# One more unit of transposes by DMA, and another order of the transfers behind the last load, in a bf16 time-mixing kernel

## The chip, the cores and the metric

One core of a Trainium2 chip runs the program. The metric is the device time of one execution in microseconds (us); before the change the median of four runs is 202.88 us (202.57 to 203.16). A smaller time is better.

## What is computed

For x of 16 batches x 2048 positions x 256 channels (f32), with x_prev the same rows shifted by one position inside a batch:

```
xv = x * time_mix_v + x_prev * (1 - time_mix_v)
xr = x * time_mix_r + x_prev * (1 - time_mix_r)
out = (sigmoid(xr @ receptance_weight) * (xv @ value_weight)) @ output_weight
```

The key path of the reference doesn't reach the output, and the kernel doesn't compute it.

## The kernel before, in words

**Units.** The work is cut into 64 units of 512 positions (NU = 64), four to a batch, so that unit 44 is the first of batch 11. In the main loop (L522) step g computes unit g: on TensorE (PE) the receptance matmuls into psum_r, the value matmuls into psum_v (both L287) and the output matmuls of an earlier unit into psum_o (L311); on ScalarE (ACT) the sigmoid (L535) and the copy of psum_o to o_sb (L345); on VectorE (DVE) the product z_sb (L580). psum_r, psum_v and psum_o have one buffer each, so PE can't begin the next group of a kind before ACT or DVE has read the last one.

**Mixing.** The matmuls need the channels on the partitions. `xt[b]` holds batch b transposed, in 17 slots of 128 columns for 128 positions x 2 channel halves: slots 1 to 16 are the batch's rows p*16+j by their j, and slot 0 holds the x_prev of slot 1, which is slot 16 moved by one column. The mixed input is a scaled slice of `xt` (DVE L257, POOL L267, and from unit 40 on for the value half ACT L514) plus the slice one slot further (DVE L279). Mixing works on pairs of units and runs one to three units ahead of the matmuls. Slot 0 is made from slot 16: for batches 11 to 15 by a small copy on ACT (L550) in step 4*(b-1)+1, so for batch 11 in step 41, for batch 12 in step 45 and for batch 14 in step 53. ACT takes its instructions in order.

**Two ways to transpose.** For the first 44 units PE transposes x_bf against an identity (L207, eight 128x128 matmuls for a unit) and ACT copies the result to `xt` (L223). The last five batches (BYDMA = 20 units) are transposed from x_bf to `xt` by DMA (`by_dma`, L188, the crossbar). `advance` runs the transposes some six units ahead; because CROSS = 38 is subtracted once in its limit, they stand in steps 36 (unit 42) and 38 (unit 43), and none in step 37. Within a batch from 2 on a unit's transposes are taken in the order of slots 13-16, 1-4, 5-8, 9-12, so unit 43 brings slots 9 to 12 of batch 10 (j = 8 to 11).

**Queues.** SyncE (SP) issues all crossbar transfers and nearly all stores, in program order, to one hardware queue. Loads of x go by POOL's queue. The last load (batch 15) is in two halves. A store moves two units (1 MB); some are kept back (WAITING) so that they don't stand among the transposes. Behind the last loads SP's order is: store of units 32-33 once the first half of the last load has landed; then, once the second half has landed, batch 11 in two transfers (slots 13-16, then 1-12), batch 12, the store of units 34-35, batch 13, four stores, batch 14, batch 15, four stores and so on. Batch 11 is issued in step 38, batches 12, 13, 14 and 15 in steps 39, 43, 47 and 51. `o_sb` and `xt` have three buffers, one batch each.

**Other names that hang on CROSS.** From step LATE_O + 1 = 39 on the output matmuls of unit g-2 stand at the start of step g, where before it those of unit g-1 stood at its end; step 38 has none. From FREE = 38 on ACT scales one channel half of the value input, for even units, in even steps.

Of the kernel before, what the change touches and what calls it, by code (L numbers as in the profile page):

```python
# [15 lines left out]
def kernel(  # L16
# [25 lines left out]
    nc = tc.nc  # L42

    B, S, D = x.shape
    P = 128
    KO = D // P
    J = S // P
    UJ = 4
    TU = UJ * P
    UB = J // UJ  # L50
# [2 lines left out]
    BYUNIT = 2  # L53
    LONG = 8
    H = UJ // 2
    BYDMA = 5 * UB
    CROSS = NU - BYDMA - LOOK
    FREE = CROSS
    LATE_O = CROSS
    WAITING = {33: 38, 35: 39, 37: 43, 39: 43, 45: 51, 47: 51}  # L60
    START_T = [1, 3, 5, 6, 7, 9, 11, 12]
    AHEAD = 6
    PAIRS = 10
# [18 lines left out]
    kept = {}  # L82
# [20 lines left out]
    def load(b):  # L103
        if b not in x_bf:
            x_bf[b] = xpool.tile([P, J, D], BF16, name="x_bf")
        if b < BYUNIT:
            for e in range(UB):
                nc.gpsimd.dma_start(
                    out=x_bf[b][:, e * UJ : (e + 1) * UJ, :], in_=unit_rows(x, b, e)[:, 0]
                )  # L110
            return
        if b < B - 1:
            run = 8192 if b < LONG else 16384
            return nc.gpsimd.dma_start(out=x_bf[b], in_=rows(b), max_dma_last_dim=run)  # L114
        return [
            nc.gpsimd.dma_start(out=x_bf[b][:, j : j + J // 2], in_=rows(b)[:, j : j + J // 2])
            for j in (0, J // 2)
        ]
# [67 lines left out]
    def by_dma(b, lo, hi, after=None):  # L186

        op = nc.sync.dma_start_transpose(  # L188
            out=xt[b][:, 1 + lo : 1 + hi].rearrange("p j k c -> p (j k) c"),
            in_=x_bf[b][:, lo:hi].rearrange("p j d -> p (j d)"),  # L190
        )
        if after is not None:
            tc.add_manual_dep(op.ins, after.ins.name, SYNC, reason="not beside a load")

    def transposes(i):

        b, e = divmod(i, UB)
        if b > 0 and e == 0:
            new_xt(b)
        if b >= BYUNIT:  # L200
            e = (e - 1) % UB
        j0 = 1 + e * UJ + (e if b < BYUNIT else 0)
        if b < BYUNIT or e == UB - 1:
            late_copies.append((b, e))

        def one(ps, jj, ko, src, idn):
            nc.tensor.transpose(  # L207
                out=ps[:, jj], in_=src[:, jj, ko * P : (ko + 1) * P], identity=idn
            )

        if i in (1, 2):
            for ko in range(KO):
                ps = ps_t_pool.tile([P, UJ, P], FP32, name="ps_t")
                for jj in range(UJ):
                    one(ps, jj, ko, x_unit[:, i], ident_f)
                nc.scalar.copy(out=xt[b][:, j0 : j0 + UJ, ko, :], in_=ps)
            return
        ps = ps_t_pool.tile([P, UJ, KO, P], BF16, name="ps_t")
        src = x_bf3 if b == 0 else x_bf[b][:, e * UJ : (e + 1) * UJ, :]
        for jj in range(UJ):  # L220
            for ko in range(KO):
                one(ps[:, :, ko], jj, ko, src, ident)
        nc.scalar.copy(out=xt[b][:, j0 : j0 + UJ], in_=ps)  # L223
# [71 lines left out]
    def project_unmixed(ps, mo):  # L295


        parts = [(w_prev[:, ko], ko, 0) for ko in range(KO)]
        parts += [(w_bf[:, 0, ko], ko, 1) for ko in range(KO)]
        for n, (w, ko, lo) in enumerate(parts):  # L300
            nc.tensor.matmul(
                out=ps[:, mo, :],
                lhsT=w[:, mo * P : (mo + 1) * P],
                rhs=xt[0][:, lo : lo + UJ, ko],
                start=(n == 0),
                stop=(n == len(parts) - 1),
            )
# [11 lines left out]
    def store(queue, b, lo, hi, after=None):  # L319
        dst = out[b].rearrange("(p j) d -> p j d", p=P)  # L320
        op = queue.dma_start(out=dst[:, lo:hi, :], in_=o_sb[b][:, lo:hi, :])
        if after is not None:
            tc.add_manual_dep(op.ins, after.ins.name, SYNC, reason="in turn with the last load")
# [9 lines left out]
    def output(g, z):  # L333
# [20 lines left out]
        elif e % 2 == 1:  # L354
            pair = (b, j0 - UJ, j0 + UJ)
            if g in WAITING:
                kept.setdefault(WAITING[g], []).append(pair)
            else:
# [46 lines left out]
    def pieces(g):  # L405

        b, e = divmod(g, UB)
        tile_for(g // 2)
        return [(b, m, e * TU, (e + 1) * TU) for m in range(2)]
# [21 lines left out]
            tc.add_manual_dep(op.ins, after.ins.name, SYNC, reason="one at a time")  # L431

    tnext = 1
    half_load = last_load = None

    def advance(limit):
        nonlocal tnext, half_load, last_load
        while tnext <= min(limit, NU - 1):
            b, e = divmod(tnext, UB)
            if b == 1 and e > 0:  # L440
                load(b + e + 1)
            elif b > 1 and e == 0 and b + 5 < B:
                if b == 2:
                    load(6)
                last_load = load(b + 5)
                if b + 5 == B - 1:
                    half_load, last_load = last_load
            if tnext < NU - BYDMA:
                transposes(tnext)
            tnext += 1  # L450
# [71 lines left out]
    for g in range(NU - 1):  # L522
        ps_r = ps_r_pool.tile([P, KO, TU], FP32, name="psum_r")
        if g == 0:
            project_unmixed(ps_r, 0)
            advance(1)
            project_unmixed(ps_r, 1)
            for ko in range(KO):
                wrap_slots(pieces(1)[0], ko)
                scale(pieces(1)[0], (ko,))  # L530
            last = add(pieces(1)[0])
        else:
            project(ps_r, g, 0)
        s_sb = zpool.tile([P, KO, TU], BF16, name="s_sb")
        nc.scalar.activation(out=s_sb, in_=ps_r, func=ACT.Sigmoid)  # L535
        advance(START_T[g] if g < len(START_T) else g + LOOK - (g == CROSS - 1))
        for b in range(B - 5, B):
            if g == max(UB * (b - 2) - 1, CROSS + (b > B - 5)):
                new_xt(b)
                if b == B - 5:  # L540
                    for pair in kept.pop(g):
                        store(nc.sync, *pair, after=half_load)
                    by_dma(b, J - UJ, J, last_load)
                    by_dma(b, 0, J - UJ, last_load)
                else:
                    by_dma(b, 0, J)
                for pair in kept.pop(g, []):
                    store(nc.sync, *pair)
            if g == UB * (b - 1) + 1:
                nc.scalar.copy(out=xt[b][:, 0, :, 1:P], in_=xt[b][:, J, :, 0 : P - 1])  # L550
        if LATE_O < g < NU - 2:
            output(g - 2, z_prev2)
        for p in products.get(g + 1, []):
            if g >= FREE and p[0][1] == 1:
                scale_act(p[0], (0,))
        for p in [q for q, _ in products[g]] + pooled[g]:
            last_unit_of = p[3] // TU - 1
            need = last_unit_of if p[0] < BYUNIT else min(last_unit_of + 1, UB - 1)
            assert UB * p[0] + need < tnext, (g, p, tnext)
            if g > AHEAD or p not in pooled[g]:  # L560
                wrap_slots(p)
        if g == 1:
            scale_act(pieces(2)[1], (1,))
        for p, kos in products[g]:
            if not (g - 1 >= FREE and p[1] == 1):
                scale(p, kos)
        for p in sums[g]:
            last = add(p)
        for p in pooled[g]:
            if p[0] >= BYUNIT:  # L570
                wrap_slots(p)
        ps_v = ps_v_pool.tile([P, KO, TU], FP32, name="psum_v")
        project(ps_v, g, 1)
        if g == 0:
            scale_act(pieces(1)[1], (0,))
            advance(2)
        z_sb = zpool.tile([P, KO, TU], BF16, name="z_sb")
        n = TU // 2 if g == NU - 2 else TU
        for c in range(0, TU, n):
            nc.vector.tensor_tensor(  # L580
                out=z_sb[:, :, c : c + n],
                in0=s_sb[:, :, c : c + n],
                in1=ps_v[:, :, c : c + n],
                op=ALU.mult,
            )
        for p in pooled[g]:
            wrap_slots(p, after=last)
            scale_pool(p, last)
        for p in held[g]:
            add(p)  # L590
        if z_prev is not None and not LATE_O <= g < NU - 3:
            output(g - 1, z_prev)
        if g == 1:
            advance(4)
        z_prev2, z_prev = z_prev, z_sb
# [31 lines left out]
```

## Time and profile before

| what | value |
|---|---|
| median of 4 runs | 202.88 us |
| the profiled execution's own time | 202.57 us |
| its span, first to last instruction | 200.5 us |
| granted TensorE clock | full throughout |
| PE transposes L207 | x328 |
| ACT copies of them L223 | x36 (and x5 for the first batches) |
| one ACT copy of psum_o, L345 | 1018 ns |
| crossbar transfers L188 | x6 |
| HBM read and written | 34.34 MB and 33.55 MB |

A row of the timeline gives the start in us from the span's beginning, the duration, the engine ("SPq" is SyncE's instruction stream, where a DMA's duration is the time of its issue and not of its transfer), the line of the kernel, the operation, and out<-in by the program's names. In brackets stands how long the engine was idle before it and who released it. The ends of matmuls are modelled and overlap the next ones, so on PE the distance from one start to the next is what counts. Step g can be found by its sigmoid on ACT: step 36 at 121.98, step 37 at 125.03, step 38 at 127.63, step 41 at 135.50, step 45 at 146.03 and step 53 at 167.11.

### The profile page before, as it was taken

How to read it: one execution, taken by the hardware profiler on the slowest of the kernel's cores; microseconds unless marked ns; L12 is line 12 of the kernel's file. 1: busy time of each engine (PE TensorE's matmuls, PEld its weight loads, DVE VectorE, ACT ScalarE, POOL GpSimd, SP SyncE). 2: the span in 40 equal slices, each digit the busy share in tenths (PEclk: the TensorE clock that was granted, in tenths of full speed). 3: DMA queues.
4: the chain of work that ended last, by engine and by line, in shares of the span. 5: the costliest groups of instructions: out<-in, count | busy, mean ns of one | idle time of the engine just before them, and what ended most of it. 6: DMA issues, size and time to landing. Idle time of an engine off the chain costs nothing.

```text
span 200.5 us, 3891 instructions
## 1 busy us (share of the span) xinstructions
PE 195.3 (97%) x1422; PEld 125.7 (63%) x1422; DVE 186.0 (93%) x296; ACT 180.3 (90%) x202; POOL 83.7 (42%) x115
## 2 busy tenths in 40 slices
PE   8999999999999999999999999999999999999993
PEld 6666676666666666666666666655666565555671
DVE  0999999999999999999999999999999999999982
ACT  3599899999999999999999999899999999999982
POOL 1756572443543534425433354443344444444200
PEclk9999999999999999999999999999999999999999
DMA  5999999999999999999999999899999999999575
GB/s 155 301 175 216 234 279 273 280 281 274 293 311 292 288 280 284 291 280 278 289 288 337 289 409 285 284 193 232 280 270 420 310 224 279 417 422 391 222 308 215
DMA packets 32298, 57.26 MB, mean 286 GB/s; under 512 B 21780, under 2 KB 23064, under 8 KB 28312
## 3 DMA queue, kind: packets, MB, share of 16 engines
q1 hardware_dynamic: 28208, 40.77, 59.7%
q0 software_dynamic: 3920, 16.12, 40.0%
q8 instruction: 11, 0.18, 0.4%
q10 hardware_dynamic: 152, 0.13, 0.2%
q14 instruction: 7, 0.06, 0.1%
HBM read 34.34 MB, written 33.55 MB: 339 GB/s over the span
## 4 chain that ended last, share of the span: by engine, by line
PE 84%; DMA 5%; DVE 5%; issue 2%; ACT 2%; POOL 0%; SPq 0%; DVEq 0%
PE psum_v L287 25%; PE psum_o L311 25%; PE psum_r L287 24%; PE ps_t L207 8%; DMA x_bf<-in_x_dram 3%; DMA w_f<-n_receptance_weight_dram 2%; DVE z_sb L580 2%; DVE mix L279 2%; PE ps_t L311 1%; DVE mix L257 1%; ACT s_sb L535 1%; ACT mix L514 1%; ACT xt L223 1%; PE ps_t L287 0%; SPq L128 0%
## 5 line engine op out<-in xcount | busy, mean ns | idle before, releaser
L267 POOL TENSOR_SCALAR mix<-xt,c_sb 128x1024 bf16<-128x1024 bf16 (+1 forms) x55 | 61.0, 1109 | 92.6 <-DVE mix L279 80.6
L580 DVE TENSOR_TENSOR z_sb<-s_sb,psum_v 128x1024 bf16<-128x1024 bf16 (+1 forms) x64 | 76.7, 1200 | 3.9 <-PE psum_v L287 1.5
L279 DVE TENSOR_TENSOR mix<-mix,xt 128x1024 bf16<-128x1024 bf16 x112 | 77.0, 696 | 1.6
L287 PEld LDWEIGHTS <-w_bf 128*128 128x128 bf16 x516 | 48.7, 98 | 38.3 <-issue 0.7
L535 ACT ACTIVATE s_sb<-psum_r 128x1024 bf16<-128x1024 f32 x63 | 65.0, 1032 | 3.5 <-PE psum_r L287 2.7
L345 ACT COPY o_sb<-psum_o 128x1024 f32<-128x1024 f32 x60 | 61.1, 1018 | 7.2 <-PE psum_o L311 7.0
L287 PE MATMUL psum_v<-mix,w_bf 128*128 128x512 bf16 (+1 forms) x256 | 65.3, 377 | 0.3 <-DVE z_sb L580 0.2
L287 PE MATMUL psum_r<-mix,w_bf 128*128 128x512 bf16 (+1 forms) x252 | 64.2, 377 | 0.1
L311 PE MATMUL psum_o<-wo_bf,z_sb 128*128 128x256 bf16 x486 | 63.2, 273 | 0.0
L311 PEld LDWEIGHTS <-z_sb 128*128 128x128 bf16 x512 | 49.8, 98 | 20.5 <-issue 1.4
L223 ACT COPY xt<-ps_t 128x1024 bf16<-128x1024 bf16 x36 | 36.6, 1029 | 0.0
L207 PEld LDWEIGHTS <-x_bf 128*128 128x128 bf16 x328 | 21.4, 98 | 9.4 <-POOL xt_first L426 0.9
L207 PE MATMUL ps_t<-ident,x_bf 128*128 128x128 bf16 x328 | 24.5, 219 | 0.4 <-DMA x_bf<-in_x_dram 0.4
L257 DVE TENSOR_SCALAR mix<-xt,c_sb 128x1024 bf16<-128x1024 bf16 (+1 forms) x49 | 22.1, 459 | 0.0
L514 ACT ACTIVATE mix<-xt,c_sb 128x1024 bf16<-128x1024 bf16 x12 | 13.9, 1157 | 0.0
L279 DVE TENSOR_TENSOR mix<-mix,xt_first 128x1024 bf16<-128x1024 bf16 x15 | 10.5, 707 | 0.1
L114 POOL DMA_DIRECT2D x_bf<-in_x_dram x13 | 8.5, 656 | 0.0
L257 DVE TENSOR_SCALAR mix<-xt_first,c_sb 128x512 bf16<-128x512 bf16 x22 | 6.7, 353 | 0.2
L223 ACT COPY xt_first<-ps_t 128x1024 bf16<-128x1024 bf16 x5 | 5.2, 1031 | 0.0
L153 PE MATMUL ps_t<-zeros 128*128 128x128 bf16 x33 | 3.5, 291 | 1.0 <-DVE zeros L90 1.0
L427 POOL COPY xt_first<-xt_first 128x254 bf16<-128x254 bf16 x5 | 2.0, 393 | 5.8 <-DVE mix L279 5.7
L267 POOL TENSOR_SCALAR mix<-xt_first,c_sb 128x512 bf16<-128x512 bf16 x6 | 4.1, 685 | 0.6
(66 smaller groups left out, 51.5 us busy)
## 6 DMA issues: line engine op xcount, KB each, us to landing
out_dram<-o_sb SPq DMA_DIRECT2D x28, 1024.0 KB, 14.1
x_bf<-in_x_dram POOLq DMA_DIRECT2D x13, 1024.0 KB, 23.9
out_dram<-o_sb SPq DMA_DIRECT2D x4, 512.0 KB, 2.8
out_dram<-o_sb SPq DMA_DIRECT2D x6, 256.0 KB, 2.5
x_bf<-in_x_dram POOLq DMA_DIRECT2D x5, 256.0 KB, 7.1
o_sb<-in_x_dram SPq DMA_DIRECT2D x2, 512.0 KB, 5.0
x_bf<-in_x_dram POOLq DMA_DIRECT2D x2, 512.0 KB, 10.9
o_sb<-in_x_dram SPq DMA_DIRECT2D x2, 256.0 KB, 3.0
```

Of the source, the lines that this page charges most:

```text
L114: return nc.gpsimd.dma_start(out=x_bf[b], in_=rows(b), max_dma_last_dim=run)
L207: nc.tensor.transpose(out=ps[:, jj], in_=src[:, jj, ko * P : (ko + 1) * P], identity=idn)
L223: nc.scalar.copy(out=xt[b][:, j0 : j0 + UJ], in_=ps)
L257: nc.vector.tensor_scalar(out=mixed(piece)[:, :, ko], in0=xt[b][:, slots(piece), ko], scalar1=c_sb[:, m, ko : ko + 1], scalar2=None, op0=A ...
L267: op = nc.gpsimd.tensor_scalar(out=mixed(piece)[:, :, 1], in0=xt[b][:, slots(piece), 1], scalar1=c_sb[:, m, 1:2], scalar2=1.0, op0=ALU.mul ...
L279: return nc.vector.tensor_tensor(out=mixed(piece), in0=mixed(piece), in1=xt[b][:, slots(piece, 1)], op=ALU.add)
L287: nc.tensor.matmul(out=ps[:, mo, :], lhsT=w_bf[:, m, ko, mo * P : (mo + 1) * P], rhs=mixed((b, m, e * TU + lo, e * TU + hi))[:, :, ko], st ...
L311: nc.tensor.matmul(out=ps[:, slot, :], lhsT=z[:, ko, jj * P : (jj + 1) * P], rhs=wo_bf[:, ko, :], start=(ko == 0), stop=(ko == KO - 1),)
L345: nc.scalar.copy(out=o_sb[b][:, j0 : j0 + UJ, :], in_=ps)
L514: nc.scalar.activation(out=mixed(piece)[:, :, ko], in_=xt[b][:, slots(piece), ko], func=ACT.Copy, scale=c_sb[:, m, ko : ko + 1],)
L535: nc.scalar.activation(out=s_sb, in_=ps_r, func=ACT.Sigmoid)
L580: nc.vector.tensor_tensor(out=z_sb[:, :, c : c + n], in0=s_sb[:, :, c : c + n], in1=ps_v[:, :, c : c + n], op=ALU.mult,)
```

## The change

BYDMA grows from 20 to 21, which makes CROSS, FREE and LATE_O 37. Unit 43 (slots 9-12 of batch 10) is now a crossbar transfer, and PE's transposes stand in steps 35 and 37, none in 36. In step 37 SP gets, behind the whole last load: slots 9-12 of batch 10, all of batch 11 in one transfer, the store of units 32-33. In step 39 it gets the store of units 34-35 and then batch 12. Batch 13 follows in step 43 with no store between. The stores kept for step 43 and everything behind stay as they were. The store of units 32-33 no longer waits for the first half of the last load but stands behind batch 11.

```diff
-    BYDMA = 5 * UB
+    BYDMA = 5 * UB + 1
     CROSS = NU - BYDMA - LOOK
     FREE = CROSS
     LATE_O = CROSS
-    WAITING = {33: 38, 35: 39, 37: 43, 39: 43, 45: 51, 47: 51}
+    WAITING = {33: CROSS, 35: CROSS + 2, 37: 43, 39: 43, 45: 51, 47: 51}
...
                 if b + 5 == B - 1:
-                    half_load, last_load = last_load
+                    last_load = last_load[-1]
...
         for b in range(B - 5, B):
-            if g == max(UB * (b - 2) - 1, CROSS + (b > B - 5)):
+            if g == max(UB * (b - 2) - 1, CROSS + 2 * (b > B - 5)):
                 new_xt(b)
                 if b == B - 5:
-                    for pair in kept.pop(g):
-                        store(nc.sync, *pair, after=half_load)
-                    by_dma(b, J - UJ, J, last_load)
-                    by_dma(b, 0, J - UJ, last_load)
-                else:
+                    by_dma(b - 1, J - 2 * UJ, J - UJ, last_load)
+                    by_dma(b, 0, J, last_load)
+                elif b > B - 4:
                     by_dma(b, 0, J)
                 for pair in kept.pop(g, []):
                     store(nc.sync, *pair)
+                if b == B - 4:
+                    by_dma(b, 0, J)
```

More of the change, by code (lines that the diff above doesn't have):

```diff
@@ L433 @@
     tnext = 1
-    half_load = last_load = None
+    last_load = None
     def advance(limit):
-        nonlocal tnext, half_load, last_load
+        nonlocal tnext, last_load
         while tnext <= min(limit, NU - 1):
```

## The prediction

> **What bounds the kernel now.** First the page: the share of busy time and the chain that ended last.
>
> ```profile
> PE 195.3 (97%) x1422; PEld 125.7 (63%) x1422; DVE 186.0 (93%) x296; ACT 180.3 (90%) x202; POOL 83.7 (42%) x115
> ...
> PE 84%; DMA 5%; DVE 5%; issue 2%; ACT 2%; POOL 0%; SPq 0%; DVEq 0%
> ```
>
> PE carries 84% of the chain, but DVE and ACT are at 93% and 90%: a wait on either reaches PE soon. So I read the stretch that the change touches (steps 35 to 53), engine by engine. PE, from the timeline:
>
> ```profile
> 123.92 1.03 PE L287 MATMUL psum_r<-mix,w_bf 128*128 128x512 bf16 x4
> 124.78 1.03 PE L287 MATMUL psum_v<-mix,w_bf 128*128 128x512 bf16 x4
> 125.65 1.04 PE L311 MATMUL psum_o<-wo_bf,z_sb 128*128 128x256 bf16 x8
> 126.52 1.03 PE L287 MATMUL psum_r<-mix,w_bf 128*128 128x512 bf16 x4
> 127.38 0.61 PE L207 MATMUL ps_t<-ident,x_bf 128*128 128x128 bf16 x8
> 127.83 1.03 PE L287 MATMUL psum_v<-mix,w_bf 128*128 128x512 bf16 x4
> ```
>
> From start to start each group takes 0.87, the transposes of a unit 0.45 (127.38 to 127.83). A unit is 2.60 on PE without transposes and 3.05 with them; the sigmoids show the same (121.98 to 125.03 in the first phase; 143.17 to 153.71, four units in 10.54, in the second). Step 37 to 41 isn't pure PE, as the chain in order of time shows:
>
> ```profile
> 127.63 0.45 ACT s_sb L535
> 128.07 0.47 issue
> 128.54 1.02 ACT xt L223
> 129.56 1.04 ACT mix L514
> 130.60 0.92 ACT s_sb L535
> 131.53 0.04 issue
> 131.57 1.02 PE psum_r L287 x4
> ```
>
> In step 38 ACT has the copy of the last PE transposes and its first scaling between two sigmoids, and PE's psum_r waits until 131.57.
>
> Then ACT around step 41, where batch 11's slot 0 is made:
>
> ```profile
> 135.50 1.01 ACT L535 ACTIVATE s_sb<-psum_r 128x1024 bf16<-128x1024 f32 x1
> 136.41 0.40 ACT L550 COPY xt<-xt 128x254 bf16<-128x254 bf16 x1
> 136.70 1.02 ACT L345 COPY o_sb<-psum_o 128x1024 f32<-128x1024 f32 x1
> 137.87 1.02 ACT L535 ACTIVATE s_sb<-psum_r 128x1024 bf16<-128x1024 f32 x1
> ```
>
> PE's next output group starts at 137.77, 0.05 after the o_sb copy ends (136.70 + 1.02): it waits for psum_o. So the slot copy is already on PE's path: slot copy start + 1.36 = output group of unit 40. It has no slack to give.
>
> Last the crossbar's rows, each asked for in its own stretch of SP's timeline:
>
> ```profile
> 128.48 1.34 SPq L188 DMA_TRANSPOSE xt<-x_bf  x1
> ```
> ```profile
> 129.88 4.10 SPq L188 DMA_TRANSPOSE xt<-x_bf  x1
> ```
> ```profile
> 134.14 4.86 SPq L188 DMA_TRANSPOSE xt<-x_bf  x1
> ```
>
> These are batch 11's slots 13-16, its slots 1-12, and batch 12. The landing counts put the first at 132.09, the second at 135.59, the third at 140.91. The slot copy of step 41 needs only slot 16, and so only the first: it was over four us early.
>
> **Part 1: a unit fewer on PE and ACT.** Removed: eight matmuls, 0.45 of PE, and one ACT copy of 1.02. The remaining transposes move to steps 35 and 37, so that ACT's copy no longer stands in the step of its first scaling, and the 0.2 to 0.3 that PE loses at 131.57 and around it goes too. I carried the order through with 0.87 a group, with the sigmoid, o_sb and z_sb durations of the rows: psum_v of step 41 would start at 135.18 instead of 135.94. DVE's z_sb then ends just in time twice (129.9 for 129.98, 135.2 for 135.18), so the value is 0.7, with bounds 0.4 (the PE time alone) and 0.75. Moving LATE_O is in that order already; FREE moves nothing, since ACT's scaling falls on even steps and the first is 38 both times. The memset of batch 11's slot (0.11 on POOL, which idles over 1 us in each step) costs nothing.
>
> **Part 2: two crossbar transfers behind the load.** The wait for the last half load releases SP at 128.48. The store of units 32-33 no longer stands beside that half load; does it come sooner? In the packet records the DMA engine that finishes the load last runs its last packets back to back (127.06, 127.36, 127.68, each 0.32), none of the store's between, so I leave 128.48 (a gain of 0.6 at most, if all the load's tail were contention; a loss has no reason).
> - Four slots of batch 10: issued 128.48 to 129.82, landed by 131.4 to 131.7. First users: POOL's scaling in step 39 (131.74 before, some 131.1 after) and ACT's in step 40. POOL's wait of half a us is covered by its own idle time (1.2 to 1.7 a step), and DVE adds that product only after 135. Cost 0.
> - All of batch 11: issued from 129.88. Batch 12's row gives 4.86 for the same shape, so until 134.74; the second part of batch 11 took 0.4 more than its share of that, so 135.1 is the other end. From end of issue to landing it was 1.61 (second part of 11) and 1.91 (batch 12). That is 136.35 to 137.0; I take 136.8.
>
> Here is the added wait. One transfer means one landing, so the slot copy of step 41, which would start at 136.41 - 0.7 = 135.7, now waits for all 16 slots until 136.8 + 0.1. Behind it in ACT's order stand the o_sb copy of unit 39 and the sigmoid of step 42; PE's output group of unit 40 waits for that copy, and with it everything that PE has queued. It starts at 136.9 + 1.36 = 138.26, where before it was 137.77: 0.49 later. The whole 0.7 is lost and 0.5 more. From there each step follows as before, since PE was back to back behind that point.
>
> A rule of the Trainium skill speaks against this sum. Rows first, the busy time by stretch (the last column is GB/s; the first stretch holds only crossbar traffic, the second mostly stores):
>
> ```profile
> 136.00:140.00 4.00, 4.00 (x24) 2.15 (x23) 3.83 (x7) 3.85 (x6) 1.12 (x2) 1.00 1.14 217
> 149.00:152.00 3.00, 3.00 (x22) 1.83 (x19) 3.00 (x5) 3.00 (x4) 1.17 (x2) 1.00 0.93 388
> ```
>
> "Advanced Engine Details and Errata", section "X-Bar Transpose (TRN2)", has transposing DMAs as fast as regular ones, 350 to 400 GB/s. The 20 columns of slots are 1.31 MB: at 375 they take 3.5, at the row's 217 they take 6.0. By the rule batch 11 would land near 134.3, ahead of its slot copy, and the change would gain its 0.7. The row decides: 217.
>
> **Part 3: the stores behind batch 11, batch 12 behind both.** The store of units 32-33 goes out at 135 instead of 125.1. Its buffer is next written by ACT for unit 44, after 149; it lands near 139.5, cost 0. But batch 12 now stands behind two stores. From its landing to that of the store behind it batch 12 shows 3.0 (140.91 to 143.89), a second store in a row 2.43 (152.98 to 155.41); batch 14, behind stores, lands 4.6 after the last of them (160.27 to 164.85). So batch 12 lands about 10.1 to 10.3 after batch 11: 147.0. Its slot copy was at 146.94 and is pushed by part 2 to 147.43: slack 0.3, cost 0. It had six us. Above, if batch 12 takes batch 13's 5.3 behind a store, or the second store 2.7, the cost is 0.5. Batch 13 needs to be there only at 157.5, batch 14 at 168.0 + 0.5: from batch 12's landing to batch 14's I count 19.6 to 20.9 against 21.1 between their slot copies. Later stores run 2.6 late, and their buffers have over 2 us.
>
> **Sum.** Against the profiled execution (span 200.5, own time 202.57): -0.7 + 1.2 + 0 = +0.5, 203.06. The median of the four runs stands 0.31 above that execution, so 203.4.
>
> **The rivals.**
> - *A, the forecast*: batch 11 lands at 136.4 to 137.2 and sets the pace: 203.4 (203.0 to 203.8). For it: the rows of issue and landing. Chance 0.50.
> - *B, faster*: batch 11 is there when its slot copy wants it. Place: ACT in step 41. The point from which it decides: a landing at 136.3 loses and gains nothing, one at 135.6 or earlier has the full gain of 0.7. For it: the packets of batch 11's first part had the tail of the store of units 32-33 among them (until 130.4), and that tail is gone; without any tail and with a load that ends 0.6 earlier the landing is 135.7. Against it: issuing alone takes until 134.7. 202.88 - 0.6 = 202.3. Chance 0.15.
> - *C, batch 12 too*: the two stores make it miss step 45 as well, 0.5 on top: 203.9 (203.5 to 204.5). For it: a slack of 0.3 on a chain of 10. Chance 0.25.
> - *D, a wash*: landing at 136.3, what is saved is lost: 202.9. Chance 0.10.
>
> **How the numbers follow.** 0.2% is 0.41, about what a measurement of this kernel can tell from no change. Slower by more: 0.65 of A (its +0.5 lies close to the bound) and nearly all of C, 0.565. Within: the rest of A, D, and scraps, 0.305. Faster: most of B, 0.13. The range 202.3 to 204.3 cuts off the lower half of B and the end of C, together not much over 0.1.
>
> **What would show it.** Right: six crossbar issues still, L207 x320; on ACT in step 41 an idle gap of about 1 us before L550, released by the DMA, then PE's psum_o of unit 40 near 138.3; psum_v of step 41 near 135.2, ahead of before. The slot copy of step 45 without a gap, or with one (C). Wrong: no gap at L550 in step 41 and the sigmoid of step 42 near 137.2 (B); SP released by the last load well before 128; a gap on POOL in step 39 that DVE feels; a wait for a store's landing on ACT's L345 in steps 46 to 58.

## The result and the profile after

The changed kernel takes 203.63 us (median of 43 runs, 202.47 to 204.84); the kernel before, on the same chips, 202.9 (64 runs). The ratio is 1.003, with a 95% interval of 1.002 to 1.004: slower by 0.6 us; 203.4 was forecast. (The two medians differ by 0.73, the two means by 0.60.) Of the kernel before, 36 of the 64 executions took less than 203 us; of the changed one, 4 of the 43. Its profiled execution took 204.04, with a span of 202.0.

That profile doesn't show the gap that I had forecast. ACT around step 41, from the timeline:

```profile
137.00 1.02 ACT L535 ACTIVATE s_sb<-psum_r 128x1024 bf16<-128x1024 f32 x1
137.90 0.41 ACT L550 COPY xt<-xt 128x254 bf16<-128x254 bf16 x1
138.20 1.03 ACT L345 COPY o_sb<-psum_o 128x1024 f32<-128x1024 f32 x1
139.34 1.02 ACT L535 ACTIVATE s_sb<-psum_r 128x1024 bf16<-128x1024 f32 x1
```

No bracket stands at L550: nothing waited. The landing count of batch 11 ends at 136.86, as forecast (136.8), but the sigmoid of step 41 is at 137.00 and not 135.50. This execution was late from the start, as PE's timeline of the first 20 us shows (before has the same group at 7.54, without a wait):

```profile
9.47 1.09 PE L207 MATMUL ps_t<-ident_f,o_sb 128*128 128x128 f32 x8 [1.70 <-DMA o_sb<-in_x_dram]
```

The second unit of x landed at 9.42 instead of 7.49 and everything on the engines came 1.76 later (the sigmoid of step 28 at 99.37, before 97.61). The load stream didn't: the first crossbar transfer went out at 128.00, before at 128.48. Was the slowdown only this late start, or was the forecast wait hidden by it? That is what the experiments had to tell.

One more thing differs. Part of PE's gain is missing. DVE in steps 36 to 38, from the timeline:

```profile
124.81 1.22 DVE L580 TENSOR_TENSOR z_sb<-s_sb,psum_v 128x1024 bf16<-128x1024 bf16 x1
125.95 0.68 DVE L279 TENSOR_TENSOR mix<-mix,xt 128x1024 bf16<-128x1024 bf16 x1
126.55 0.22 DVE L427 COPY xt<-xt 128x254 bf16<-128x254 bf16 x1
126.69 0.48 DVE L257 TENSOR_SCALAR mix<-xt,c_sb 128x1024 bf16<-128x1024 bf16 x1
127.27 0.69 DVE L279 TENSOR_TENSOR mix<-mix,xt 128x1024 bf16<-128x1024 bf16 x1
127.88 1.21 DVE L580 TENSOR_TENSOR z_sb<-s_sb,psum_v 128x1024 bf16<-128x1024 bf16 x1
129.01 1.02 DVE L279 TENSOR_TENSOR mix<-mix,xt 128x1024 bf16<-128x1024 bf16 x1
129.96 0.47 DVE L257 TENSOR_SCALAR mix<-xt,c_sb 128x1024 bf16<-128x1024 bf16 x1
130.35 0.68 DVE L279 TENSOR_TENSOR mix<-mix,xt 128x1024 bf16<-128x1024 bf16 x1
130.95 1.21 DVE L580 TENSOR_TENSOR z_sb<-s_sb,psum_v 128x1024 bf16<-128x1024 bf16 x1
```

From z_sb to z_sb it is 3.07 twice, and no row shows a wait. In before the second of the two takes 2.83 (126.39 to 129.22); the difference is the add at 129.01, 1.02 instead of 0.78. POOL's scaling runs beside it until 129.50. It came late because it waited for ACT's copy of PE's last transposes, which now stand in step 37:

```profile
128.38 1.12 POOL L267 TENSOR_SCALAR mix<-xt,c_sb 128x1024 bf16<-128x1024 bf16 x1 [2.26 <-ACT xt L223]
```

The add ends 0.53 after that scaling. This is no accident: from 20 us on, in all fourteen profiles, every add of L279 that took more than 0.72 began beside a POOL scaling and ended 0.53 to 0.55 after it (238 adds). What holds it is not shown. PE, in the next row, waits for the last z_sb to free psum_v:

```profile
132.22 1.02 PE L287 MATMUL psum_v<-mix,w_bf 128*128 128x512 bf16 x4 [0.21 <-DVE z_sb L580]
```

### The profile page after: what moved, and what is told of

Its sections match the earlier page's. It is cut to its first block, busy times and chain, and to the rows that moved or that the text cites. A ratio compares the mean times of both kernels' runs of the same rounds, so it can differ in the third digit from the quotient of the medians.

```text
span 202.0 us, 3877 instructions
## 1 busy us (share of the span) xinstructions
PE 195.2 (97%) x1414; PEld 125.6 (62%) x1414; DVE 186.5 (92%) x296; ACT 179.2 (89%) x201; POOL 83.8 (41%) x115
## 4 chain that ended last, share of the span: by engine, by line
PE 82%; DVE 8%; DMA 4%; issue 2%; SPq 1%; POOL 1%; ACT 1%; DVEq 0%; POOLq 0%
PE psum_v L287 25%; PE psum_o L311 24%; PE psum_r L287 23%; PE ps_t L207 7%; DMA w_f<-in_value_weight_dram 4%; DVE mix L279 3%; DVE z_sb L580 2%; DVE mix L257 2%; PE ps_t L311 1%; POOL mix L267 1%; ACT s_sb L535 1%; PE ps_t L287 0%; SPq L128 0%; DVE w_bf L470 0%; SPq L134 0%
## 5 line engine op out<-in xcount | busy, mean ns | idle before, releaser
L279 DVE TENSOR_TENSOR mix<-mix,xt 128x1024 bf16<-128x1024 bf16 x112 | 77.3, 699 | 1.6
L535 ACT ACTIVATE s_sb<-psum_r 128x1024 bf16<-128x1024 f32 x63 | 64.9, 1031 | 4.3 <-PE psum_r L287 3.6
L223 ACT COPY xt<-ps_t 128x1024 bf16<-128x1024 bf16 x35 | 35.6, 1030 | 0.0
L207 PE MATMUL ps_t<-ident,x_bf 128*128 128x128 bf16 x320 | 23.9, 219 | 0.0
L279 DVE TENSOR_TENSOR mix<-mix,xt_first 128x1024 bf16<-128x1024 bf16 x15 | 10.6, 715 | 0.1
L216 ACT CAST xt_first<-ps_t 128x512 bf16<-128x512 f32 x4 | 2.1, 588 | 3.2 <-PE ps_t L207 3.2
```

The costliest lines, as they stand in the source:

```text
L207: nc.tensor.transpose(out=ps[:, jj], in_=src[:, jj, ko * P : (ko + 1) * P], identity=idn)
L279: return nc.vector.tensor_tensor(out=mixed(piece), in0=mixed(piece), in1=xt[b][:, slots(piece, 1)], op=ALU.add)
```

## The experiments

Because the start of compute moves from one execution to the next, I compare profiles from the sigmoid of step 28 on (rows of ACT's timeline, L535). Steps 28 to 36 take 24.37 or 24.38 in every kernel. All in us, up to the sigmoid of the step named; "first crossbar" is the issue of the first transfer of L188.

| kernel | step 28 at | first crossbar | wait of ACT's slot copy | steps 36-42 | 42-62 | 62 to end | 28 to end | ratio to before (95%) |
|---|---|---|---|---|---|---|---|---|
| before | 97.61 | 128.48 | 0 | 15.89 | 53.53 | 9.06 | 102.85 | |
| before_again | 98.70 | 127.95 | 0 | 15.89 | 53.55 | 9.06 | 102.87 | 1.0008 (0.9989 to 1.0028) |
| before_late | 98.78 | 128.47 | 0 | 15.89 | 53.54 | 9.08 | 102.88 | 1.0003 (0.9981 to 1.0026) |
| before_plus1 | 97.59 | 128.71 | 0 | 15.89 | 53.54 | 9.49 | 103.29 | 1.0015 (0.9994 to 1.0036) |
| order_only | 97.71 | 128.05 | 0 | 15.89 | 53.53 | 9.13 | 102.92 | 1.0005 (0.9980 to 1.0031) |
| after | 99.37 | 128.00 | 0 | 15.59 | 53.57 | 9.13 | 102.67 | 1.003 (1.002 to 1.004) |
| after_again | 98.16 | 128.57 | 0.89, step 41 | 16.38 | 53.84 | 9.35 | 103.94 | 1.0034 (1.0013 to 1.0055) |
| after_late | 97.70 | 128.70 | 1.44, step 41 | 16.94 | 53.78 | 9.65 | 104.74 | 1.0048 (1.0026 to 1.0071) |
| t10_only | 97.22 | 128.99 | 0 | 16.39 | 53.87 | 9.53 | 104.16 | 1.0038 (1.0018 to 1.0059) |
| split | 97.80 | 128.48 | 0.83, step 45 | 15.69 | 54.79 | 9.56 | 104.41 | 1.0053 (1.0032 to 1.0075) |
| split_t12 | 97.52 | 127.93 | 0 | 15.59 | 53.84 | 9.62 | 103.42 | 1.0013 (0.9985 to 1.0041) |
| noskip_split_t12 | 97.44 | 128.57 | 0 | 16.13 | 54.02 | 9.86 | 104.38 | 1.0043 (1.0023 to 1.0064) |
| best_a | 98.95 | 128.20 | 0 | 15.59 | 53.57 | 9.29 | 102.82 | 1.0030 (1.0011 to 1.0049) |
| t10_twice | 97.98 | 127.74 | 3.03, step 41 | 18.52 | 55.35 | 9.52 | 107.76 | 1.0228 (1.0185 to 1.0271) |

Read the second and third columns first: step 28 falls anywhere from 97.2 to 99.4, the first crossbar transfer between 127.7 and 129.0, and the two don't move together. The theories: **W**, batch 11's late landing holds its slot copy, and with it PE; **S**, only the start was late; **O**, the new order of the stores costs; and later **E**, something at the end.

**after_again** and **before_again**: both kernels unchanged.

> The changed kernel once more, for a second profile. Theory W (batch 11 lands as one transfer at 136.8 and its slot copy on ACT in step 41 waits for it): 203.4 to 203.7; where the kernel starts as early as before did (sigmoid of step 28 near 97.6), a gap of 0.5 to 1.2 us before L550 in step 41. Rival S (the difference comes from the start: in the profile of after the second x unit and the value weights landed 1.9 us later, and all steps with them): 203.4 to 203.7 too, but the sigmoid of step 28 again near 99 and no gap before L550.

> The kernel before, submitted like a changed one. W and S both: ratio 1.000, 202.9. W allows a late start here too (sigmoid of step 28 between 97.6 and 99.4, the time following it one to one); S expects the early start, near 97.6.

The second profile of the changed kernel shows the forecast gap. ACT, and PE behind it:

```profile
135.79 1.02 ACT L535 ACTIVATE s_sb<-psum_r 128x1024 bf16<-128x1024 f32 x1
137.71 0.40 ACT L550 COPY xt<-xt 128x254 bf16<-128x254 bf16 x1 [0.89 <-DMA xt<-x_bf]
138.02 1.01 ACT L345 COPY o_sb<-psum_o 128x1024 f32<-128x1024 f32 x1
138.92 1.03 ACT L535 ACTIVATE s_sb<-psum_r 128x1024 bf16<-128x1024 f32 x1
```
```profile
139.07 1.03 PE L311 MATMUL psum_o<-wo_bf,z_sb 128*128 128x256 bf16 x8 [0.98 <-ACT o_sb L345]
```

ACT waits 0.89 for the DMA (batch 11 landed at 137.68) and PE waits 0.98 for ACT's next copy. S falls: this start was 1.2 earlier than in the first profile, and the time is no shorter. before_again starts late too (98.70), and there all that follows is as in before: S's early start for before was wrong as well.

**before_late** and **after_late**: `WARM2 = 10` becomes 28, 18 more dummy matmuls on PE.

> Before, with 18 more of the dummy matmuls on PE ahead of step 0 (28 instead of 10): compute starts some 1.5 us later, the loads don't. Both theories: 1.2 to 1.6 over before, 204.2 to 204.5, without a gap at L550.

> After, with the same 18 dummy matmuls. W (the crossbar's clock is the end of the load stream near 128, whatever compute does, and so a late compute finds batch 11 landed): no gap before L550 in step 41, and the order turns round: 0.1 to 0.3 under before_late, 204.0 to 204.3. If the cost of the change were work on the engines or a slower queue: 0.6 over before_late, 204.9.

As a delay they could not be relied on: before_late's ratio is 1.0003. In its profile PE comes to the second unit of x at 8.87, 1.3 later than in before and without a wait for the load; in after_late's it comes at 7.92, just after the unit landed (7.88). So the test of the turned order was not made. But after_late gave a third profile of the same main loop, with an early start, and the largest gap:

```profile
135.33 1.02 ACT L535 ACTIVATE s_sb<-psum_r 128x1024 bf16<-128x1024 f32 x1
137.80 0.40 ACT L550 COPY xt<-xt 128x254 bf16<-128x254 bf16 x1 [1.44 <-DMA xt<-x_bf]
```

Start 99.37, 98.16, 97.70: wait 0, 0.89, 1.44. The slot copy ran at 137.71 and 137.80 in the two that waited. The spans are 202.0, 202.1 and 202.4, whenever compute began; those of before, before_again and before_late follow the start (200.5, 201.6, 201.7). In these three an early start is waited away. They don't stand for every execution: the timed ones of the changed kernel have spans from 200.5 to 202.8.

**order_only**: 20 units by crossbar, with the new order.

```diff
-    BYDMA = 5 * UB + 1
+    BYDMA = 5 * UB
...
-    WAITING = {33: CROSS, 35: CROSS + 2, 37: 43, 39: 43, 45: 51, 47: 51}
+    WAITING = {33: CROSS, 35: CROSS + 1, 37: 43, 39: 43, 45: 51, 47: 51}
...
-            if g == max(UB * (b - 2) - 1, CROSS + 2 * (b > B - 5)):
+            if g == max(UB * (b - 2) - 1, CROSS + (b > B - 5)):
...
-                    by_dma(b - 1, J - 2 * UJ, J - UJ, last_load)
```

> After without the extra unit: 20 units by crossbar as before (unit 43 by PE, steps 36 and 38), but the new order: batch 11 in one transfer behind the whole last load, stores of units 32-33 and 34-35, batches 12 and 13 as one block. W (20 columns of slots ahead of batch 11's landing are what makes it late): batch 11 lands 1.2 us earlier, near 135.6, its slot copy in step 41 wants it at 136.4, batch 12 lands near 145.8 against 146.9: no gap, ratio 1.000. Rival O (the new order alone costs): a gap before L550 in step 41 or 45 and 1.002 to 1.004.

```profile
135.60 1.01 ACT L535 ACTIVATE s_sb<-psum_r 128x1024 bf16<-128x1024 f32 x1
136.51 0.40 ACT L549 COPY xt<-xt 128x254 bf16<-128x254 bf16 x1
```

No wait with an early start (97.71), and up to step 62 each stage is that of before. O falls, as far as this profile goes (the ratio's interval, up to 1.0031, would leave room for it): one transfer for batch 11, the moved stores and the block of batches 12 and 13 cost nothing as long as the four extra slots aren't ahead of them. Its first crossbar transfer went out 0.5 to 0.65 earlier than in the two profiles that wait. That alone doesn't explain the missing wait: its issue ended at 132.98, and with 0.65 more and the 2.74 from there to the landing that after_late shows, I estimate 136.4, still ahead of the copy at 136.51, though barely.

**t10_twice**: the line of `by_dma(b - 1, ...)` stands twice.

> After with the transfer of slots 9-12 of batch 10 made twice, the same data to the same place: a known delay of 1.2 to 1.4 us ahead of batch 11. W: the gap before L550 in step 41 grows by that, and the time with it: 1.2 over after, near 204.8, ratio 1.009. S, or a cost that lies on the engines: no more than 0.2 over after.

The wait grew to 3.03 and the time (six executions) by 4.4 over after, not by 1.2. The second copy was not issued until the first had landed (its issue is at 130.92, where the next transfer went out at 130.08 in after_again), and POOL waited for it too:

```profile
134.32 2.92 POOL L267 TENSOR_SCALAR mix<-xt,c_sb 128x1024 bf16<-128x1024 bf16 x2 [3.43 <-DMA xt<-x_bf]
```

Behind the wait PE was also slower for a while. The page's row of the granted TensorE clock (40 slices of 5.1 us, in tenths) has one slice well below 9. It begins at 138.9, and in it two PE groups took 1.86 and 1.81 instead of 1.03; the rows of before, after, after_again and after_late have no such slice:

```profile
PEclk9999999999999999999999999996999999999999
```
```profile
141.03 1.86 PE L311 MATMUL psum_o<-wo_bf,z_sb 128*128 128x256 bf16 x8 [2.15 <-ACT o_sb L345]
142.69 1.81 PE L287 MATMUL psum_v<-mix,w_bf 128*128 128x512 bf16 x4
```

Step 42 took 4.52, in after_again 3.18. The direction is W's; the size is not a measure of one transfer.

**t10_only**: before, with unit 43's transfer added.

```diff
-    BYDMA = 5 * UB
+    BYDMA = 5 * UB + 1
...
-    WAITING = {33: 38, 35: 39, 37: 43, 39: 43, 45: 51, 47: 51}
+    WAITING = {33: 37, 35: 39, 37: 43, 39: 43, 45: 51, 47: 51}
...
+                    by_dma(b - 1, J - 2 * UJ, J - UJ, last_load)
                     by_dma(b, J - UJ, J, last_load)
```

> Before, with nothing changed but unit 43 going by crossbar (behind the last load, ahead of batch 11 in two transfers); the stores of units 32-33 and 34-35 keep their old places. W: the gain of the dropped PE transposes without the wait, 202.4 to 202.8. S: as after if the start is late for every kernel with the new constants, 203.5. If it is slower than before without a late start, the transfer of slots 9-12 itself or the moved transposes cost, and POOL or DVE shows a wait in steps 37 to 41.

Slower, and not by the slot copy. With the store of units 32-33 ahead of it, the transfer of slots 9-12 landed at 132.40 (start 97.22, the earliest of all), and POOL's scaling began only at 132.58. DVE's scaling beside it took 1.35 instead of 0.47, and in step 41 PE waited 0.64 for the z_sb that came after:

```profile
132.58 1.42 POOL L267 TENSOR_SCALAR mix<-xt,c_sb 128x1024 bf16<-128x1024 bf16 x1 [2.44 <-DVE z_sb L581]
```
```profile
132.93 1.35 DVE L257 TENSOR_SCALAR mix<-xt,c_sb 128x1024 bf16<-128x1024 bf16 x1
```

(The first row names the z_sb that ended at 132.41; in the changed kernel the same scaling begins 0.2 behind that z_sb's start, at 133.54, so it is the landing that was late.) So the wait had another place; the expectation of a gain was wrong.

**split**: batch 11 in two transfers, slots 13-16 first.

```diff
-                    by_dma(b, 0, J, last_load)
+                    by_dma(b, J - UJ, J, last_load)
+                    by_dma(b, 0, J - UJ, last_load)
```

> After, with batch 11 again in two transfers, slots 13-16 ahead of slots 1-12; all else as in after. W: the slot copy of step 41 waits for a transfer that lands near 133 and no longer stalls; 202.5 to 202.8, some 0.3 under before, because the profile of after shows PE's 0.9 gained by step 39 and 0.65 of it lost to DVE there. S: no change from after, 203.5. A third, C (batch 12 behind two stores misses step 45): a gap before L550 in step 45 instead, 203.2 to 203.6.

Slots 13-16 alone landed at 133.50. The gap of step 41 is gone and step 45 has it, as rival C of the prediction had it (batch 12 landed at 148.16); the expectation's 202.5 to 202.8 was missed (204.24):

```profile
148.19 0.40 ACT L551 COPY xt<-xt 128x254 bf16<-128x254 bf16 x1 [0.83 <-DMA xt<-x_bf]
```

**split_t12**: split, with the two stores behind batch 12 (`33: CROSS + 2`, and batch 12's `by_dma` ahead of the pop of kept stores).

> Split, with batch 12 right behind batch 11 and the stores of units 32-33 and 34-35 behind batch 12 (before batch 13). W with C (in split the wait moved to batch 12 in step 45): both slot copies on time, batch 11's slots 13-16 near 133.5, batch 12 near 142.5; what stays is DVE's 0.65 in step 39 and POOL's wait for slots 1-12: 202.7 to 203.1, ratio 0.999 to 1.001. If O or something at the end of the kernel costs, 1.003 as in split.

Steps 36 to 42 take 15.59, 0.30 under before, and neither slot copy waits. POOL waits for slots 1-12:

```profile
137.32 1.12 POOL L267 TENSOR_SCALAR mix<-xt,c_sb 128x1024 bf16<-128x1024 bf16 x1 [1.77 <-DMA xt<-x_bf]
```

and step 43 takes 0.26 more; the add of DVE that begins beside this scaling, at 137.83, takes 1.15. From step 28 to the end it is 0.57 over before; the rest of that is at the end (9.62), which led to E.

**noskip_split_t12**: `advance(... g + LOOK)` without `- (g == CROSS - 1)`.

> Split_t12, with PE's transposes in steps 35 and 36 and none in step 37, so that POOL has unit 42 a step earlier. If DVE's 0.65 in step 39 comes from POOL waiting for unit 42's copy in step 37: step 39 takes 2.2 to 2.4 instead of 2.79, and the time is 0.3 to 0.5 under split_t12, 202.3 to 202.7. If DVE is simply full there, step 39 stays at 2.79 or the loss shows in step 38, and nothing is gained.

Step 39 fell from 2.78 to 2.37, as the idea had it: POOL's scaling of unit 42 now comes at 126.47, and the add beside it takes 0.78. But step 36 rose from 2.60 to 3.05, and steps 36 to 39 sum to 10.4 in both. That loss is on PE, where two psum_r groups now stand with only psum_v between them:

```profile
125.94 1.02 PE L287 MATMUL psum_r<-mix,w_bf 128*128 128x512 bf16 x4 [0.30 <-ACT s_sb L535]
```

From one of these psum_r to the next it is 2.19 in both kernels (123.75 to 125.94; in split_t12 123.39 to 125.58), since the second needs the sigmoid of the first. With the transposes in step 37 their 0.45 lies in this interval and costs nothing; in step 36 it is on top. So POOL's late unit 42 does cost step 39 its 0.4, and bringing it forward costs the same elsewhere. The steps behind were slower by waits for DMA.

**before_plus1**: before, with one store made as two.

```diff
-                        store(nc.sync, *pair, after=half_load)
+                        store(nc.sync, pair[0], pair[1], pair[1] + UJ, after=half_load)
+                        store(nc.sync, pair[0], pair[1] + UJ, pair[2], after=half_load)
```

> Before, with the store of units 32-33 made as two stores of one unit: one DMA more on SP's queue and nothing else. Theory E (at the end SP waits for a fixed list of semaphores one after another at 0.06 us each; the stores take eight semaphores in turn, and one DMA more or less decides whether the last store's semaphore is the last on the list or the first): from the sigmoid of step 62 to the end 9.5 instead of 9.06, 0.4 over before, 203.3, ratio 1.002. If the longer end of split, t10_only and split_t12 (9.53 to 9.62) came from stores that lag behind: 9.06 and ratio 1.000.

E holds in the profile: 9.49, all else as in before; the ratio (1.0015) is too wide to say. SP's own waits from 196 on, before and then before_plus1 (L622 and L623 stand for the end of the program):

```profile
SPq L622 <- DMA out_dram<-o_sb: 1.2, 3, 0.8
```
```profile
SPq L623 <- DMA out_dram<-o_sb: 1.6, 1, 1.6
```

In before the waits at the end are three, as the stores land; with one DMA more the last store has the semaphore that stands first among the eight of the list, and the other seven, long there, are still gone through behind it at 0.06 each, 0.43 in all. This 0.43 is in split, t10_only, split_t12 and noskip_split_t12, which issue one DMA more. The changed kernel issues as many as before: none of its loss is E.

**best_a**: batch 11 by due time, two whole-batch stores.

```diff
-                    by_dma(b, 0, J, last_load)
+                    by_dma(b, J - UJ, J, last_load)
+                    by_dma(b, 0, J - 2 * UJ, last_load)
+                    by_dma(b, J - 2 * UJ, J - UJ, last_load)
...
-                for pair in kept.pop(g, []):
+                both = kept.pop(g, [])
+                if len(both) == 2 and g < UB * (B - 4):
+                    both = [(both[0][0], 0, J)]
+                for pair in both:
                     store(nc.sync, *pair)
```

> A version made from the runs: unit 43 by crossbar as in after; batch 11 in three transfers by their due times (slots 13-16, 1-8, 9-12), batch 12 right behind, then the stores of units 32-35 as one store of the whole batch and, behind batch 13, units 36-39 likewise, so that the count of DMAs stays that of before. W and E: no gap at L550 in steps 41 and 45, POOL and DVE without a wait for slots 1-8 (landed near 135), end of 9.06 to 9.3; 0.1 to 0.3 under before, 202.6 to 202.8, ratio 0.999. If the store queue's lag at the end costs as in after_again (9.35), 1.000.

In its profile nothing waits for a DMA between 126 and 155, and 28 to end is 102.82, as before; but this start was late (98.95), and the timed ratio is 1.0030, where 0.999 was expected. I have no profile of it with an early start, so where it loses then stays open. No version with the extra unit beat the kernel before; split_t12 alone can't be told from it.

## Why the prediction was right, and which terms were not

- **The wait of part 2** is what happens: ACT's slot copy waited for batch 11 in the two profiles in which compute wasn't late. That the extra unit is the cause is shown by order_only, where the four slots are not there and nothing waits, and by t10_twice, where they stand twice and the wait is 3.03.
- **217 GB/s against the rule of the skill** (the Trainium skill, "Advanced Engine Details and Errata", section "X-Bar Transpose (TRN2)": 350 to 400): the row held. Batch 11's issue took 4.69 to 4.88, against 4.86 for the same shape in before, and 133 to 135 in after_again moved 217 GB/s. At the rule's rate the prediction's estimate of the landing, 134.3, would have meant no wait and a gain.
- **The landing itself was mis-sized.** In after_again and after_late the transfers went out 0.1 and 0.2 later than the 128.48 taken, but batch 11 landed 0.9 and 1.0 later than the 136.8 taken, at 137.68 and 137.78. From the end of its issue it took 2.72 and 2.74, where 1.61 to 1.91 had been read from before. A landing is counted sixteen times; fifteen counts were in at 137.08 and 137.17, and the last came 0.6 later. In before batch 13 shows the same, 149.20 and then 150.74, and the prediction's "5.3 behind a store" for it is the time of the fifteenth: with the last it is 6.85. What delays the last one is open.
- **The 0.7 of part 1 was mis-sized**: steps 36 to 42 gain 0.30 when nothing waits (after, split_t12, best_a). The step that failed is "DVE's z_sb then ends just in time twice": PE's psum_v came at 132.22, where 0.87 behind the group at 130.96 would have been 131.83, so 0.39 of the gain went there. The prediction had followed what the move of the transposes to step 37 does for ACT, and not what waits for their copy: POOL's scaling, and with it DVE's add of 1.02.
- **The price of the wait**, 1.2 in the forecast, was 1.0 in after_again, whose compute started 0.55 later than in before's profile, and 1.5 in after_late, which started as early: step 41 was longer by 0.79 and 1.34, and step 42 by 0.2 in both. That 0.2 I had not forecast; ACT, just released, waits for PE there:

```profile
140.14 1.01 ACT L345 COPY o_sb<-psum_o 128x1024 f32<-128x1024 f32 x1 [0.20 <-PE psum_o L311]
```
- **"Their buffers have over 2 us" was right of the buffers and missed the end.** The store queue itself runs behind. Busy time by stretch, before and then after_again (last columns: DMA share, GB/s):

```profile
188.50:192.50 4.00, 4.00 (x27) 2.43 (x25) 3.67 (x6) 3.70 (x5) 0.07 (x1) 1.00 0.61 245
```
```profile
188.50:192.50 4.00, 4.00 (x28) 2.59 (x27) 3.97 (x6) 4.00 (x6) 1.12 (x1) 1.00 1.01 398
```

In before the stores have caught up ten us before the end; in the changed kernel the DMA is still full, and step 62 to the end takes 0.07, 0.29 and 0.59 more in the three profiles. The last store takes 2.04 from issue to landing in before, and 2.08, 2.33 and 2.63 in the three, so the longer end is its landing. No run changed the store queue alone.
- **Rival C** was there, hidden: batch 12 landed at 148.1 for a slot copy at 148.2 to 148.4. It takes over when the first wait is removed (split).
- **Not thought of**: the start of compute varies by two us against the load stream, so the price depends on the execution: -0.2, +1.1, +1.9 from step 28 on against before. The measured 0.6 lies between. That the total came so near is luck. My +0.5 was -0.7 + 1.2 for an execution that starts as early as the profile of before did; such a one (after_late) has -0.3 + 1.3 + 0.2 in steps 36 to 42 and 0.6 at the end, each term worse than forecast, and loses 1.9. What brings the median down, as far as the profiles show, is that other executions start later and wait less or not at all. Three profiles don't tell how often each happens.

## What to carry to other kernels

Work moved from a busy engine to a queue is due at a time that the queue sets, not the engine: ask what the queue's clock is (here the end of the loads) and how much is left between its landing and the first reader. Merging transfers makes the most urgent reader wait for the least urgent bytes (slots 13-16 landed at 133.50 by themselves, the whole batch at 137.68). Moving an instruction to help one engine moves what waits for it: follow the next reader too, and look at what then runs beside what. Compare stages from a common mark inside the loop, and take more than one profile: one late start hid the wait altogether.

## What the runs showed of the hardware that I had not expected

- The first loads don't land at the same time in each execution: the second unit of x at 7.49 and 8.88 in two profiles of the kernel before, at 9.42, 8.31 and 7.88 in three of the changed one, whose start is the same.
- A DVE add from two SBUF tiles that begins while a POOL scaling runs ends 0.53 to 0.55 after it: 1.02 beside the scaling at 128.38, up to 1.53 in after_late, and 0.69 without one.
- The last of a crossbar transfer's sixteen counts can come late by itself: 0.6 after the others in after_again, 1.54 in before (batch 13).
- After a wait of PE of 2.15 the granted clock fell for one slice and a group took 1.86 instead of 1.03 (t10_twice); after 0.98 it didn't (after_again). Where between the two it starts wasn't measured.
- The waits at the end of the program go through a fixed list at 0.06 each, so one DMA more moved the end by 0.43 (9.06 to 9.49).
